# mLSTM head selectors made one head ahead, head 0's products of values spread over more steps, and a last norm in three vector steps with one product on GpSimd

## The chip, the cores and the metric

The kernel runs on one core of one Trainium2 chip. The time is device time of one execution in microseconds (us). The engines are TensorE (PE, matmuls), VectorE (DVE), ScalarE (ACT), GpSimd (POOL) and SyncE (SP, which issues DMAs here). In the code `T`, `V`, `S`, `G` and `nc.sync` stand for them in that order.

## The reference

A decoder block on 512 tokens of 1024 features with 16 learned tokens ahead, all in float32: a norm, one wide projection, an mLSTM mixer and a gated linear attention (GLA) mixer of 4 heads each beside each other, a gated merge, an output projection, a SwiGLU channel mixer, and a last norm. What the change touches is the mLSTM mixer and the last norm:

```python
dmat = jnp.where(causal, b[..., :, None] - b[..., None, :] + logi[..., None, :], -jnp.inf)
...
m_row = jnp.maximum(inter_log, jnp.max(dmat, axis=-1))
sim = jnp.einsum('bhcjd,bhcsd->bhcjs', q, k)
wts = jnp.exp(dmat - m_row[..., None]) * sim
...
den = a_inter * jnp.einsum('bhcd,bhcjd->bhcj', ns, q) + jnp.sum(wts, axis=-1)
return num / jnp.maximum(jnp.abs(den), jnp.exp(-m_row))[..., None]
...
out = rmsnorm(h, final_g)     # h * rsqrt(mean(h*h) + EPS) * final_g
```

## The kernel before, in words

Features lie on the 128 partitions and tokens along the free axis. A float32 product is made of three products of rounded halves: every weight is split into a high part (`whi`, a cast on ACT, L188) and a low part (`wlo`, a subtraction on DVE, L193), and so are the inputs. The projections of the mLSTM heads come first, one block of 128 columns after the other (`mm3`, L302 to L304). The later projections come in pairs by a scheme with seven products in place of eight (`seven` and `pair`, L344 to L346), in the order p7, q1, p3 of the pair before, q6, p4, p2, q5, of 12 matmuls each per half of the inner dimension. q1, q6 and q5 run in the same bank `bx`: between them ACT copies it out (`s1` L404 after q1, `s2` L405 after q6, `s5` L406 after q5), and the next of the three waits for its copy. `s7` (L407) and `c12` (L409) are two more such copies.

The order on every engine is the order in which the program is written; nothing reorders it. What lies beside the projections is written as generators: each `tick()`, called between the projections' matmuls (some 0.7 us of PE apart), moves every generator in `side` on by one step, and of the list `mixers` only the first, which holds the mLSTM heads 0 to 3 and then the GLA heads. `yield n` leaves n ticks before the next step. An earlier step of one head therefore brings forward all that follows in `mixers`, and its place among the projections with it.

All matmuls write into one pool of 8 banks of PSUM, taken by `bank()` in the program's order; a matmul into a bank waits until what the bank held before was read out. SBUF tiles of a tag wait in the same way.

A head (`mlstm`, L867) waits for its gates, queries and keys. It then makes a selector `sel` (L872), a matrix that picks this head's rows of the gate sums `gts.R`; two products with it (L875, L876) spread two gate rows over all partitions (`pb`, `pm`). ACT copies `pb` into `nml` (L879), DVE adds the causal mask (`dia`, L880), and for each of five chunks PE makes the scores (`sp`, L897 to L899), ACT the exponentials, DVE their product (L904), ACT and DVE its two halves `wh` and `wl` (L908, L917). When the values are there (transposed by PE, L748 and L766, read out by L752, L757, L769 and L774) follow the two halves of the product of values (`num`, L939 to L941), with the row sums (`den`, L944, L945) between, and the head's norm (`head_out`), which takes one more sum `ss` (L808, L809). `dh` and `dl` (L925, L930) are the halves of the row sums' input. The gates themselves come from `gate_rows`, which runs once, ahead of head 0; the convolution of queries and keys is L716.

`final(a, o)` is the last norm of column half a. `ones` times the squares gives their sum in a bank; ACT makes Ln and Exp (both L132, the line of the helper `act`) as a first guess of the inverse root, DVE improves it by a Newton step (L1488 to L1491), multiplies four blocks of two features each (L1495) and sends each off by a DMA (L1497). Half 0 runs while PE makes the last projection's second half; half 1 ends the program.

Of the kernel before, what the change touches and what calls it, by code (L numbers as in the profile page):

```python
# [9 lines left out]
F32R = mybir.dt.float32r  # L10
I32 = mybir.dt.int32
AF = mybir.ActivationFunctionType
ALU = mybir.AluOpType
PSUM = bass.MemoryType.PSUM

P = 128
D = 1024
KT = 8
NM = 16
NS = 512  # L20
NT = NM + NS
HALF = NT // 2
H = 4
DFF = 2816
FT = DFF // P
EPS = 1e-6
# [64 lines left out]
def jrange(c):  # L91
    return max(0, CH * c - NM), min(NS, CH * c + CH - NM)
# [8 lines left out]
def hybrid_block(ctx: ExitStack, tc: tile.TileContext, xT, wst, par, con, out):  # L101
    nc = tc.nc
    V, S, G, T = nc.vector, nc.scalar, nc.gpsimd, nc.tensor
# [3 lines left out]
    def nm(s):  # L107
        cnt[0] += 1
        return f"{s}_{cnt[0]}"
# [6 lines left out]
    def tt(dt=F32, n=NT, p=P):  # L116
        t = tpool.tile([P, TW], dt, tag="t", name=nm("t"))
        return t[:p, :n]

    def bank():  # L120
        return psum.tile([P, 512], F32, tag="b", name=nm("b"))
# [4 lines left out]
    def act(o, i, func, **kw):  # L126
        want = TABLE.get(func)
        if want is not None and want != table[0]:
            if want == LOGEXP:
                S.preload_act_table_set(want)  # L130
            table[0] = want
        S.activation(o, i, func, **kw)  # L132
# [288 lines left out]
    for k in range(KT):  # L421
        t = tt()
# [18 lines left out]
    cn = apool.tile([P, NS + 8], F32, name="cn")  # L441
# [3 lines left out]
    mpool = mpool_stack.enter_context(tc.tile_pool(name="mpool", bufs=1))  # L445
# [20 lines left out]
    for k in range(KT):  # L466
        g = pr[:, C_N1 + k:C_N1 + k + 1]
# [156 lines left out]
    gts = Box()  # L624
    gts.ready = False

    def gate_rows(ps):
        a2s = gts.a2s = apool.tile([P, 512], F32R, name="a2s")
        a2f = pr[:, C_A2:C_A2 + 512]
        gsb = tt()  # L630
        for a in range(2):
            c = slice(a * HALF, (a + 1) * HALF)
            V.tensor_tensor(gsb[:96, c], ps[0][a][:96], rstd[:96, c], ALU.mult)
        yield 16
        gam = gts.gam = tt(F32R)
        S.copy(gam[:96], gsb[:96])
        bi = pr[0:32, C_BG:C_BG + 1]
        bf = pr[32:64, C_BG:C_BG + 1]
        r1, r2, bl, a0 = tt(p=32), tt(p=32), tt(p=32), tt(p=32)
        act(r1, gsb[32:64], AF.Abs, bias=bf)  # L640
        yield 1
        act(r1, r1, AF.Exp, scale=-1.0)
        V.tensor_scalar(r2, gsb[32:64], bf, 0.0, op0=ALU.add, op1=ALU.min)
        yield 1
        act(r1, r1, AF.Ln, bias=b_one[:32])
        V.tensor_tensor(gam[64:96], gsb[64:96], gam[64:96].bitcast(F32), ALU.subtract)
        S.copy(a2s[:96], a2f[:96])
        yield 1
        V.tensor_tensor(r2, r2, r1, ALU.subtract)
        V.tensor_tensor_scan(bl, rmask[:32], r2, 0.0, ALU.mult, ALU.add)  # L650
        yield 1
        V.tensor_tensor(a2s[32:64], a2f[32:64], a2s[32:64].bitcast(F32), ALU.subtract)
        V.scalar_tensor_tensor(a0, gsb[0:32], bi, bl, ALU.add, ALU.subtract)
        yield 1
        d0, ml = r1, r2
        V.memset(d0, 0.0)
        V.tensor_copy(d0[:, CH::CH], bl[:, CH - 1:NT - 1:CH])
        V.tensor_tensor_scan(ml, d0, a0, 0.0, ALU.add, ALU.max)
        yield 1
        R = gts.R = tt(F32R, NS)  # L660
        mr = tt(p=32)
        rhi = d0
        act(R[0:32], ml[:, NM:], AF.Copy, scale=-1.0)
        V.tensor_tensor(mr, ml, bl, ALU.add)
        V.tensor_scalar(mr, mr, -1.0, 40.0, op0=ALU.mult, op1=ALU.min)
        yield 1
        V.scalar_tensor_tensor(R[32:64], ml[:, NM:], -1.0, R[0:32].bitcast(F32), ALU.mult, ALU.subtract)
        S.copy(R[64:96], mr[:, NM:])
        yield 1
        S.copy(rhi[:, NM:], R[64:96].bitcast(F32))  # L670
        yield 1
        V.tensor_tensor(R[96:128], mr[:, NM:], rhi[:, NM:], ALU.subtract)

        acol = gts.acol = apool.tile([P, 480], F32, name="acol")
        gts.idx = {}
        rows = [a0]
        n_ix = 0
        for d in range(NCK):
            if d > 0:
                nxt = tt(p=32)  # L680
                for i in range(NCK - d):
                    e = CH * (i + d) - 1
                    V.tensor_scalar(nxt[:, CH * i:CH * i + CH], rows[-1][:, CH * i:CH * i + CH], bl[:, e:e + 1],
                                    None, op0=ALU.add)
                rows.append(nxt)
            yield 2
        yield 8
        pst = bank()
        for d in range(NCK):
            n_ix = gate_cols(pst, rows, d, n_ix)  # L690
            yield 1
        yield 2
        V.tensor_copy(acol, pst[:, :480])
        gts.ready = True

    def gate_cols(pst, rows, d, n_ix):
        for i in range(NCK - d):
            w0, w1 = kwin(i)
            T.transpose(pst[:, n_ix * 32:n_ix * 32 + 32], rows[d][:, w0:w1], ident[:32, :32])
            gts.idx[(d, i)] = n_ix  # L700
            n_ix += 1
        return n_ix
# [161 lines left out]
    WTOT = off  # L864


    def mlstm(h, q, k, v, gates, dst):  # L867
        while not gts.ready or q.v is None or k.v is None:
            yield 1
        (qh, ql), (kh, kl) = q.v, k.v  # L870
        sel = mpool.tile([P, 2, P], F32R, tag="sel", name=nm("sel"))
        S.copy(sel, cn[:, NS + h:NS + 8:H].unsqueeze(2).to_broadcast([P, 2, P]))  # L872
        yield 6
        pb, pm = bank(), bank()
        T.matmul(pb, sel[:, 0], gts.R, start=True, stop=True)  # L875
        T.matmul(pm, sel[:, 1], gts.R, start=True, stop=True)  # L876
        yield 1
        nml, dia, em = tt(n=NS), tt(n=NS), tt(n=NS)
        S.copy(nml, pb)  # L879
        V.tensor_tensor(dia, pb, mask, ALU.add)  # L880
# [9 lines left out]
        for i in range(NCK + 1):  # L890
            cur = None
            if i < NCK:
                j0, j1 = jrange(i)
                w0, w1 = kwin(i)
                n = NS - j0
# [4 lines left out]
                e = tt(n=n)  # L900
# [27 lines left out]
        vh, vl = v.v  # L928
        yield 2
        V.tensor_tensor(dl, es, dh.bitcast(F32), ALU.subtract)  # L930
        yield 6
        den = bank()
        num = [bank(), bank()]
        for vt in range(2):
            for i in range(NCK):
                j0, o = jrange(i)[0], WOFF[i]
                n = NS - j0
                fi, la = i == 0, i == NCK - 1
                T.matmul(num[vt][:, j0:], vh(i, vt), wh[:, o:o + n], start=fi, stop=False)  # L939
                T.matmul(num[vt][:, j0:], vh(i, vt), wl[:, o:o + n], start=False, stop=False)  # L940
                T.matmul(num[vt][:, j0:], vl(i, vt), wh[:, o:o + n], start=False, stop=la)  # L941
            yield 1
            if vt == 0:
                T.matmul(den, onesr, dh, start=True, stop=False)  # L944
                T.matmul(den, onesr, dl, start=False, stop=True)  # L945
                act(nml, den, AF.Abs)
                yield 1
                V.tensor_tensor(em, nml, em, ALU.max)
                act(em, em, AF.Square)
# [156 lines left out]
    def head(kind, h):  # L1106
        if (kind, h) not in heads:
            b = heads[kind, h] = Box()
            b.q, b.k, b.v, b.vf, b.gates = box(), box(), box(), [box(), box()], [box(), box()]
            if kind == "m":  # L1110
                mix(mlstm(h, b.q, b.k, b.v, b.gates, ym))
                run(values(b.v, mtail, b.vf, h, True))
            else:
                dk = box()
                run(gla_decay(h, b.q, b.k, dk))
                mix(gla(h, dk, b.v, b.gates, yg))
                run(values(b.v, gtail, b.vf, h, False))
        return heads[kind, h]
# [178 lines left out]
    HS = NS // 2  # L1297
# [176 lines left out]
    def final(a, o):  # L1474
        yield 16
        ps = bank()[:, :HS]
        T.matmul(ps, ones, hsum[a].v, start=True, stop=False)
        while o.v is None:
            yield 1
        yield from out_res(7, o.v, a * HS, (a + 1) * HS)  # L1480
        yield 1
        T.matmul(ps, ones, hsum[a].w, start=False, stop=True)
        yield 1
        y, t = tt(n=HS), tt(n=HS)
        act(y, ps, AF.Ln, bias=b_eps, scale=1.0 / D)
        act(y, y, AF.Exp, scale=-0.5)
        yield 1
        V.tensor_tensor(t, y, y, ALU.mult)  # L1488
        V.scalar_tensor_tensor(t, ps, D * EPS, t, ALU.add, ALU.mult)
        V.tensor_scalar(t, t, -0.5 / D, 1.5, op0=ALU.mult, op1=ALU.add)  # L1490
        V.tensor_tensor(y, y, t, ALU.mult)  # L1491
        yield 1
        for j in range(4):
            g = hgain[j, a]
            V.tensor_tensor(g, g, y.unsqueeze(1).to_broadcast([P, 2, HS]), ALU.mult)  # L1495
            q = S if j % 2 else nc.sync
            q.dma_start(out[2 * j:2 * j + 2, :, a * HS:(a + 1) * HS].rearrange("m p n -> p m n"), g)  # L1497
            yield 1

# [109 lines left out]
```

## Time and profile before

| | |
|---|---|
| median of 3 runs | 948.26 us (947.28 to 948.26) |
| profiled execution | 948.52 us, span 946.7 us |
| granted clock of TensorE, mean | 0.992 |
| PE busy | 917.5 us, 97% of the span |
| DVE, ACT, POOL busy | 636.2, 546.2, 86.8 us |
| DMA moved | 124.45 MB, mean 131 GB/s |

In the rows below, a timeline row gives start, duration, engine, line, operation, names, tile shapes, count, and in brackets the idle time before it with what ended it. A row of waits gives the waiting line, what it waited for, total, count and longest. Times are us from the span's start.

### The profile page before, as it was taken

Reading aid. Unit: us, or ns where it says so; the run is one execution under the profiler, and the core shown is the slowest. Engines: PE = TensorE matmul, PEld = TensorE weight load, DVE = VectorE, ACT = ScalarE, POOL = GpSimd, SP = SyncE. Lnnn points to the kernel's source line nnn. Section 1 sums busy time; section 2 is a strip of 40 time slices with the busy share of each in tenths; the row PEclk is TensorE's granted clock in tenths of the full one; section 3 lists DMA queues with packets and bytes.
Section 4 is the critical chain, followed back from the end, with each engine's and each line's share of the span. In section 5 each row is a group of like instructions: output and inputs, shape, how many; then the busy total and the mean of one; then the engine's idle time right before and its main releaser. Section 6 shows DMA issues by size and latency. Waiting matters only on the chain.

```text
span 946.7 us, 15478 instructions
## 1 busy us (share of the span) xinstructions
PE 917.5 (97%) x6083; PEld 842.3 (89%) x6083; DVE 636.2 (67%) x940; ACT 546.2 (58%) x954; POOL 86.8 (9%) x102
## 2 busy tenths in 40 slices
PE   6999999989999999999999999999999999999995
PEld 6988899878998899999998888888999999888885
DVE  6797776767875577777777556785767767842323
ACT  7557788779684256766874334443555555732321
POOL 0000022001100011110100000212121110000000
PEclk9999999989999999999999999999999999999998
DMA  7245375345562466655643343335788885322302
GB/s 262 101 139 155 119 162 123 75 112 134 127 163 90 111 148 155 163 120 141 134 134 107 116 133 116 107 102 132 185 186 179 189 191 148 115 94 85 111 1 89
DMA packets 48712, 124.45 MB, mean 131 GB/s; under 512 B 5376, under 2 KB 11520, under 8 KB 48640
## 3 DMA queue, kind: packets, MB, share of 16 engines
q1 hardware_dynamic: 35008, 101.32, 34.5%
q0 software_dynamic: 12544, 21.11, 14.5%
q8 instruction: 47, 0.77, 0.3%
q10 hardware_dynamic: 1088, 1.05, 0.3%
q14 instruction: 25, 0.20, 0.1%
HBM read 118.08 MB, written 5.37 MB: 130 GB/s over the span
## 4 chain that ended last, share of the span: by engine, by line
PE 78%; ACT 9%; DVE 8%; issue 3%; DMA 1%; DVEq 0%; SPq 0%; ACTq 0%
PE b L303 13%; PE b L302 13%; PE b L304 13%; PE b L344 12%; PE b L345 11%; PE b L346 11%; ACT t L132 4%; ACT whi L188 2%; DVE wlo L193 1%; ACT L130 1%; PE b L1056 1%; DVE t L716 1%; PE b L1058 1%; PE b L1035 1%; ACT L132 1%
## 5 line engine op out<-in xcount | busy, mean ns | idle before, releaser
L303 PE MATMUL b<-t,whi 128*128 128x512 f32 (+2 forms) x822 | 289.9, 353 | 1.0 <-DVE t L471 0.7
L302 PE MATMUL b<-t,whi 128*128 128x512 f32 (+2 forms) x774 | 274.0, 354 | 6.7 <-ACT t L132 6.6
L304 PE MATMUL b<-t,wlo 128*128 128x512 f32 (+2 forms) x774 | 270.8, 350 | 0.0
L344 PE MATMUL b<-t,whi 128*128 128x256 f32 (+1 forms) x864 | 250.0, 289 | 7.7 <-ACT t L404 6.1
L346 PE MATMUL b<-t,wlo 128*128 128x256 f32 (+1 forms) x864 | 245.1, 284 | 0.0
L345 PE MATMUL b<-t,whi 128*128 128x256 f32 (+1 forms) x864 | 245.0, 284 | 0.0
L193 DVE TENSOR_TENSOR wlo<-raw,whi 128x1024 fp32r<-128x1024 f32 x155 | 193.1, 1249 | 50.8 <-ACT whi L188 50.5
L188 ACT CAST whi<-raw 128x1024 fp32r<-128x1024 f32 x155 | 161.7, 1047 | 64.5 <-PE b L345 27.4
L303 PEld LDWEIGHTS b<-t,whi 128*128 128x128 f32 x822 | 155.8, 190 | 23.3 <-DVE t L843 1.1
L344 PEld LDWEIGHTS b<-t,whi 128*128 128x128 f32 x864 | 164.3, 190 | 9.9 <-ACT t L404 7.2
L302 PEld LDWEIGHTS b<-t,whi 128*128 128x128 f32 x774 | 147.0, 190 | 26.5 <-ACT t L132 6.6
L345 PEld LDWEIGHTS b<-t,whi 128*128 128x128 f32 x864 | 164.3, 190 | 0.5
L304 PEld LDWEIGHTS b<-t,wlo 128*128 128x128 f32 x774 | 146.8, 190 | 19.9 <-DVE wlo L193 0.3
L346 PEld LDWEIGHTS b<-t,wlo 128*128 128x128 f32 x864 | 164.0, 190 | 0.0
L132 ACT ACTIVATE t<-t 128x512 f32<-128x512 f32 (+6 forms) x124 | 70.4, 588 | 29.8 <-DVE t L1289 9.3
L183 POOL DMA_DIRECT2D raw<-wst x36 | 31.2, 867 | 364.4 <-DMA wf<-wst 104.9
L188 ACT CAST whi<-wf 128x1024 fp32r<-128x1024 f32 x36 | 37.8, 1051 | 22.5 <-PE b L345 13.5
L132 ACT ACTIVATE t<-f 128x256 f32<-128x256 f32 (+1 forms) x24 | 11.6, 482 | 61.6 <-DVE f L1456 61.6
L212 POOL DMA_DIRECT2D wf<-wst x36 | 32.5, 912 | 155.3 <-DMA wf<-wst 85.7
L193 DVE TENSOR_TENSOR wlo<-wf,whi 128x1024 fp32r<-128x1024 f32 x36 | 43.9, 1218 | 0.0
L1456 DVE TENSOR_TENSOR f<-f,b 128x512 f32<-128x512 f32 (+1 forms) x9 | 5.7, 629 | 53.3 <-PE b L304 53.3
L344 PE MATMUL b<-t,wgh 128*128 128x256 f32 (+1 forms) x144 | 41.0, 285 | 0.0
(219 smaller groups left out, 1216.6 us busy)
## 6 DMA issues: line engine op xcount, KB each, us to landing
raw<-wst SPq DMA_DIRECT2D x155, 512.0 KB, 3.6
wf<-wst SPq DMA_DIRECT2D x36, 256.0 KB, 3.2
wf<-wst POOLq DMA_DIRECT2D x36, 256.0 KB, 5.4
raw<-wst POOLq DMA_DIRECT2D x36, 256.0 KB, 4.7
t<-xT SPq DMA_DIRECT2D x8, 264.0 KB, 5.6
pos<-t SPq DMA_DIRECT2D x8, 264.0 KB, 2.3
t<-xT SPq DMA_DIRECT2D x8, 256.0 KB, 3.8
t<-neg POOLq DMA_DIRECT2D x6, 272.0 KB, 6.3
```

The lines of the kernel that those rows point to most:

```text
L130: S.preload_act_table_set(want)
L132: S.activation(o, i, func, **kw)
L183: G.dma_start(lr(r, 0), lr(wst[v - 1], 0), accum_op=ALU.add)
L188: S.copy(t, src)
L193: V.tensor_tensor(t, src, hi.bitcast(F32), ALU.subtract)
L212: G.dma_start(lr(st.f, 1), lr(wst[u + 1], 1), accum_op=ALU.add)
L302: T.matmul(o, w_h, ah[:, c0:c1], start=first, stop=False)
L303: T.matmul(o, w_h, al[:, c0:c1], start=False, stop=False)
L304: T.matmul(o, w_l, ah[:, c0:c1], start=False, stop=last)
L344: T.matmul(o, h, xh_[k][:, c0:c1], start=start and k == 0, stop=False, skip_group_check=not start)
L345: T.matmul(o, h, xl_[k][:, c0:c1], start=False, stop=False, skip_group_check=not start)
L346: T.matmul(o, l, xh_[k][:, c0:c1], start=False, stop=k == 3, skip_group_check=not start)
```

## The change

`selector(h)` makes `gts.sel`, for head 0 in `gate_rows` behind `R`, for head h + 1 in head h behind its two products; the six ticks between selector and products are gone. In head 0 there are 8 ticks instead of 6 ahead of `den` and `num`, and 4 more between the halves of `num`. In `final`, the factor with the sum is made by one DVE operation beside ACT's Ln and Exp; the Newton step then takes three operations; the products are made in the order 2, 0, 1, 3, number 2 on GpSimd, and numbers 1 and 2 are sent from ACT's queue.

```diff
@@ gate_rows
         V.tensor_tensor(R[96:128], mr[:, NM:], rhi[:, NM:], ALU.subtract)
+        selector(0)
@@ mlstm
+    def selector(h):
+        gts.sel = mpool.tile([P, 2, P], F32R, tag="sel", name=nm("sel"), bufs=1)
+        S.copy(gts.sel, cn[:, NS + h:NS + 8:H].unsqueeze(2).to_broadcast([P, 2, P]))
+
...
-        sel = mpool.tile([P, 2, P], F32R, tag="sel", name=nm("sel"))
-        S.copy(sel, cn[:, NS + h:NS + 8:H].unsqueeze(2).to_broadcast([P, 2, P]))
-        yield 6
+        sel = gts.sel
         pb, pm = bank(), bank()
         T.matmul(pb, sel[:, 0], gts.R, start=True, stop=True)
         T.matmul(pm, sel[:, 1], gts.R, start=True, stop=True)
         yield 1
+        del sel
+        if h < H - 1:
+            selector(h + 1)
...
-        yield 6
+        yield 8 if h == 0 else 6
         den = bank()
         num = [bank(), bank()]
         for vt in range(2):
+            if h == 0 and vt:
+                yield 4
@@ final
+        y, t, x = tt(n=HS), tt(n=HS), tt(n=HS)
...
-        y, t = tt(n=HS), tt(n=HS)
+        V.tensor_scalar(x, ps, D * EPS, -0.5 / D, op0=ALU.add, op1=ALU.mult)
         act(y, ps, AF.Ln, bias=b_eps, scale=1.0 / D)
         act(y, y, AF.Exp, scale=-0.5)
         yield 1
         V.tensor_tensor(t, y, y, ALU.mult)
-        V.scalar_tensor_tensor(t, ps, D * EPS, t, ALU.add, ALU.mult)
-        V.tensor_scalar(t, t, -0.5 / D, 1.5, op0=ALU.mult, op1=ALU.add)
-        V.tensor_tensor(y, y, t, ALU.mult)
+        V.tensor_tensor(t, t, x, ALU.mult)
+        V.scalar_tensor_tensor(y, t, 1.5, y, ALU.add, ALU.mult)
         yield 1
-        for j in range(4):
+        for j in (2, 0, 1, 3):
             g = hgain[j, a]
-            V.tensor_tensor(g, g, y.unsqueeze(1).to_broadcast([P, 2, HS]), ALU.mult)
-            q = S if j % 2 else nc.sync
+            e = G if j == 2 else V
+            e.tensor_tensor(g, g, y.unsqueeze(1).to_broadcast([P, 2, HS]), ALU.mult)
+            q = S if j in (1, 2) else nc.sync
```

In the changed file the lines of `mlstm` stand 3 to 8 lower (pb L878, `nml` L885, `dia` L886, scores L903, casts L914, `num` L947, `den` L952), the convolution is L717, and the last products are L1504.

Three places show how the order moves. First ACT where head 0's selector was made in the kernel before; `cn` holds the constants, `b_866` is `pb`:

```order
L511 CAST t_791<-t_767 128x528
L132 ACTIVATE t_794<-t_767 128x272
L872 CAST sel_799<-cn 128x256
L752 CAST t_827<-b_816 128x512
L769 CAST t_844<-b_846 128x256
L132 ACTIVATE t_877<-t_862,pr 128x528
L879 COPY t_880<-b_866 128x512
```

and the same place in the changed kernel, where the selector is that of head 1 and `b_801` is `pb` of head 0:

```order
L511 CAST t_793<-t_769 128x528
L132 ACTIVATE t_796<-t_769 128x272
L870 CAST sel_812<-cn 128x256
L885 COPY t_814<-b_801 128x512
L130 ACT_TABLE_LOAD
L132 ACTIVATE t_816<-b_802,cb 128x512
L753 CAST t_840<-b_827 128x512
```

Head 0's own selector has gone 17 rows ahead, and the copy of `pb` stands ahead of the reading of head 1's transposed values (L753) instead of behind it.

Second ACT in the third pair, from its L404 to behind its L405. Before:

```order
L404 COPY t_2627<-b_2623 128x256
L407 COPY t_2628<-b_2622 128x256
L130 ACT_TABLE_LOAD
...
L132 ACT_TABLE_LOAD
L132 ACTIVATE t_2462<-t_2462 128x512
L132 ACTIVATE t_2463<-t_2463 128x512
L132 ACTIVATE t_2329<-b_2706 128x512
L405 COPY t_2628<-b_2623 128x272
L132 ACTIVATE t_2331<-t_2331 128x512
L130 ACT_TABLE_LOAD
```

and in the changed kernel, where `t_2758` is the norm's sum of head 3:

```order
L404 COPY t_2677<-b_2673 128x256
L407 COPY t_2678<-b_2672 128x256
L130 ACT_TABLE_LOAD
...
L132 ACT_TABLE_LOAD
L132 ACTIVATE t_2498<-t_2498 128x512
L132 ACTIVATE t_2499<-t_2499 128x512
L130 ACT_TABLE_LOAD
L132 ACTIVATE t_2599<-t_2758 128x512
L405 COPY t_2678<-b_2673 128x272
```

The reading of head 3's `den` (`b_2706`) is no longer there, and a table load and the norm's logarithm have come ahead of L405.

Third DVE in the last norm of half 1. Before:

```order
L1488 TENSOR_TENSOR t_9931<-t_9930 128x256
L1489 SCALAR_TENSOR_TENSOR t_9931<-b_9908,t_9931 128x256
L1490 TENSOR_SCALAR t_9931<-t_9931 128x256
L1491 TENSOR_TENSOR t_9930<-t_9930,t_9931 128x256
L1495 TENSOR_TENSOR t_9304<-t_9304,t_9930 128x512
L1495 TENSOR_TENSOR t_9404<-t_9404,t_9930 128x512
L1495 TENSOR_TENSOR t_9590<-t_9590,t_9930 128x512
L1495 TENSOR_TENSOR t_9772<-t_9772,t_9930 128x512
```

and in the changed kernel:

```order
L1493 TENSOR_SCALAR t_9912<-b_9909 128x256
L1497 TENSOR_TENSOR t_9911<-t_9910 128x256
L1498 TENSOR_TENSOR t_9911<-t_9911,t_9912 128x256
L1499 SCALAR_TENSOR_TENSOR t_9910<-t_9911,t_9910 128x256
L1504 TENSOR_TENSOR t_9304<-t_9304,t_9910 128x512
L1504 TENSOR_TENSOR t_9404<-t_9404,t_9910 128x512
L1504 TENSOR_TENSOR t_9772<-t_9772,t_9910 128x512
```

The third product (`t_9590`) is gone from DVE; it stands on GpSimd, behind nothing but the same product of half 0.

On PE, head 3's products with the selector and its scores stand ahead of the first pair instead of reaching into it, and its `num` and `den` in the second pair instead of the third.

## The prediction

> **What bounds the kernel now.** I read the page's busy line and chain first, then the list of what TensorE (PE) waits for, then the timeline around each of those waits.
>
> ```profile
> PE 917.5 (97%) x6083; PEld 842.3 (89%) x6083; DVE 636.2 (67%) x940; ACT 546.2 (58%) x954; POOL 86.8 (9%) x102
> PE 78%; ACT 9%; DVE 8%; issue 3%; DMA 1%; DVEq 0%; SPq 0%; ACTq 0%
> ...
> PE b L344 <- ACT t L404: 6.1, 4, 3.6
> PE b L875 <- ACT sel L872: 1.9, 1, 1.9
> PE b L939 <- DVE t L757: 1.6, 1, 1.6
> PE b L344 <- ACT t L405: 1.1, 1, 1.1
> PE b L748 <- ACT t L591: 0.5, 1, 0.5
> ```
>
> PE is busy for 917.5 of 946.7 us, so all idle time is 29.2 us, and the change can win only what PE waits for, or what lies behind PE's last product. The waits (total, count, longest) name its targets: the selector (L875), the second half of a product of values (L939), and the copies of the paired products (L404, L405), which come when head 3 ends. The profiled execution took 948.52 us (span 946.7 and 1.82 around it), 0.26 above the median of the runs, 948.26; the terms are differences against the profiled execution and are then taken from the median.
>
> **Head 0's selector.** These are rows of the timeline, of PE, DVE and ACT in turn.
>
> ```profile
> 67.20 0.28 PE L302 MATMUL b<-t,whi 128*128 128x264 f32 x1
> 69.60 0.50 PE L875 MATMUL b<-t,sel 128*128 128x512 f32 x1 [1.87 <-ACT sel L872]
> ...
> 68.72 1.53 DVE L716 SCALAR_TENSOR_TENSOR t<-t,pr,t 128x512 f32<-128x512 f32 x2
> ...
> 69.16 0.39 ACT L872 CAST sel<-cn 128x256 fp32r<-128x256 f32 x1
> ```
>
> The two products with the selector now come 12 triples of projection products earlier, near 62.4, and the wait of 1.87 is gone. But their banks must be emptied: the copy of the first (ACT, L885) stands behind the next selector's cast, which ends near 69.5, so it ends near 70.0; the masked sum (DVE, L886) stands behind L716, which ends at 70.25, so it ends near 70.9. The projection product that takes this bank ran at 67.20. With the two products with the selector (0.57) and three score products (0.69) ahead of it, and 0.7 of smaller waits for banks (pm's, and the scores' behind L593), PE reaches it near 69.15 and waits 1.75. New waits of 2.45 stand against the old 1.87 and 0.12 (at the first score product): +0.4, between −2.0 (no bank waits) and +0.9. The casts are the same four as before, at 0.39 each, in an ACT that idles there: 0.
>
> **Products of values and the transposes.** The wait at the second half of head 0's product of values:
>
> ```profile
> 104.09 0.47 PE L939 MATMUL b<-wh,t 128*128 128x512 f32 x1 [1.57 <-DVE t L757]
> ...
> 103.26 0.68 DVE L757 TENSOR_TENSOR t<-b,t 128x512 fp32r<-128x512 f32 x1
> ```
>
> Its bank is that of head 1's transposed values, read by DVE until 103.94. The longer steps (8 and 4) leave this half where it was among the projections, while the first half, den and its reading by ACT (Abs) are 3 to 5 us earlier; the bank it takes is now den's, free near 99.7. Gone: 1.57; one short wait near 97 of 0.18 goes too, and den's own second product may wait 0.2 for DVE: −1.55 (−1.75 to −0.6, the last if ACT reads den 1 us late). The wait of 0.45 at L748 goes, since its transposes now stand behind more PE work: −0.45 (0 at the other end). For heads 1 and 2 I find no wait at their places before and none after; 0, with 0.5 either way.
>
> **Head 3 and the four pairs.** Head 3's scores move from the first pairs to ahead of them, and its products of values from the third pair to the second.
>
> ```profile
> 179.90:199.30 19.40, 16.22 (x96) 14.03 (x94) 13.79 (x19) 16.52 (x31) 1.72 (x2) 0.97 0.35 86
> 199.30:214.70 15.40, 14.30 (x95) 13.91 (x95) 9.30 (x15) 10.77 (x27) 0.86 (x1) 0.81 0.34 98
> ...
> 199.71 0.58 PE L344 MATMUL b<-t,whi 128*128 128x256 f32 x1 [3.59 <-ACT t L404]
> 215.10 0.39 PE L344 MATMUL b<-t,whi 128*128 128x256 f32 x1 [1.09 <-ACT t L404]
> 221.07 0.38 PE L344 MATMUL b<-t,whi 128*128 128x256 f32 x1 [1.11 <-ACT t L405]
> 243.84 0.40 PE L344 MATMUL b<-t,whi 128*128 128x272 f32 x1 [0.88 <-ACT t L404]
> ```
>
> The columns of the windows are length, busy time (count) of PE, weight loads, DVE, ACT and GpSimd, granted clock, DMA share, GB/s. In the 19.4 us before the first copy L404 ACT works 16.5 and idles 2.9; the exponentials and casts of head 3 that move there from the next window, about 5.0 to 5.5 by their rows, fill this and 2.2 us more, so L404 comes at 201.5 instead of 199.29, and the product behind it 0.42 later, at 201.9. PE comes later too, since more of the score products (1.7) precede: at 197.8 instead of 196.1. The first wait is about 4.1 in place of 3.59, +0.5 (0 to +2, the latter if the casts wait for DVE as they do in the second window). In the second pair ACT then has 5.6 us between two L404 instead of the 10.65 it has in the second window, and PE has head 3's products between: both waits go, 1.09 + 1.11 = −2.2 (−1.1 at the worst). The fourth pair's 0.88 goes, some 0.4 of it back at a weight's low part: −0.5.
>
> The third pair had no wait, and gets one:
>
> ```profile
> 226.62 0.40 ACT L404 COPY t<-b 128x256 f32<-128x256 f32 x1
> 227.32 1.28 ACT L130 ACT_TABLE_LOAD   x1
> ...
> 230.82 1.28 ACT L132 ACT_TABLE_LOAD   x1
> ...
> 233.18 0.58 ACT L132 ACTIVATE t<-b 128x512 f32<-128x512 f32 x1
> 233.65 0.38 ACT L405 COPY t<-b 128x272 f32<-128x272 f32 x1
> ...
> 235.15 1.28 ACT L130 ACT_TABLE_LOAD   x1
> ...
> 227.99 0.39 PE L939 MATMUL b<-wh,t 128*128 128x512 f32 x1
> 232.27 0.40 PE L939 MATMUL b<-wh,t 128*128 128x512 f32 x1
> 236.81 0.29 PE L344 MATMUL b<-t,whi 128*128 128x272 f32 x1
> ```
>
> ACT is at L405 7.03 us after L404. In the changed order the activation at 233.18 is gone from between, and a table load (1.28) and a logarithm (0.53) stand there: 7.03 − 0.47 + 1.82 = 8.4, and 8.8 with L405 itself. PE needed it only at 236.81, because 4.9 us of head 3's products stood between (two halves from 227.99 and 232.27, of 15 matmuls and 2.2 us each, and den's two of 0.5). In the changed order PE has from the end of the product that L404 copies only four groups of 12 matmuls at 0.118 (24 in 2.80 us, in the row at 205.20 below) and two for a norm: 48 × 0.118 + 0.45 = 6.1. So PE waits 8.8 − 6.1 = +2.7 (0 if the copies and loads slip ahead of it, +3.5 at most, if L404 itself is late).
>
> The clock adds a risk:
>
> ```profile
> 199.50:202.00 2.50, 2.29 (x10) 2.29 (x11) 0.67 (x1) 2.29 (x8) 0.00 (x0) 0.50 1.05 235
> 202.00:205.20 3.20, 3.20 (x15) 3.01 (x15) 1.31 (x3) 0.67 (x2) 0.00 (x0) 0.51 0.29 113
> 205.20:208.00 2.80, 2.80 (x24) 2.80 (x24) 1.72 (x3) 2.38 (x5) 0.00 (x0) 1.00 0.00 0
> 70.00:74.00 4.00, 3.88 (x28) 3.49 (x27) 4.00 (x9) 0.29 (x2) 0.00 (x0) 1.00 0.58 166
> ```
>
> Behind the wait of 3.59 the clock was half for 5.5 us, a loss of 2.7; behind that of 1.87 (last row) it was full. The first wait stays long, so its loss stays; a third-pair wait of 2.7 lies between the two lengths, and I leave it at full clock. The Trainium skill ("TensorE: Matmul & The Clock Gate", What's actually happening) has the clock halved by an idle window of about 3.4 us, free-running; by that page 2.7 us would not fill one, so the sum would stand and the slower rival below would fall away, and the wait of 3.59 would fill one only where its phase is right. The row at 70 agrees for 1.87; no run here shows 2.7.
>
> **The last norm.** Only the second column half ends the program.
>
> ```profile
> 939.84 0.29 DVE L1490 TENSOR_SCALAR t<-t 128x256 f32<-128x256 f32 x1
> 940.16 0.43 DVE L1491 TENSOR_TENSOR t<-t,t 128x256 f32<-128x256 f32 x1
> 940.62 2.50 DVE L1495 TENSOR_TENSOR t<-t,t 128x512 f32<-128x512 f32 x4
> ...
> 610.38 4.55 POOL L1294 TENSOR_TENSOR t<-t,t 128x512 f32<-128x512 f32 x1 [6.64 <-ACT t L132]
> 631.56 1.59 POOL L1294 TENSOR_TENSOR t<-t,t 128x512 f32<-128x512 f32 x1 [0.71 <-DVE t L1290]
> ...
> 631.92 2.32 DVE L193 TENSOR_TENSOR wlo<-raw,whi 128x1024 fp32r<-128x1024 f32 x1
> 606.62 1.21 DVE L193 TENSOR_TENSOR wlo<-raw,whi 128x1024 fp32r<-128x1024 f32 x1
> ```
>
> L1490's place leaves the path (−0.32); its successor, read from the bank, lies beside ACT's Ln and Exp. DVE's four products of 0.62 become three, so alone they would end at 942.2 instead of 943.1. But beside a GpSimd product of 1.59 the same DVE subtraction took 2.32 instead of 1.21: it stood still until GpSimd was done. So in the tail the second DVE product waits: GpSimd 940.45 to 942.05, the second product to 942.65, the third to 943.2, as before. The tail is then +0.1; −0.7 if the two run side by side (GpSimd's transfer, then j=1's behind it on ACT's queue, set the end). In the row at 610.38 it is GpSimd that stood still, 4.55 us behind five back-to-back DVE operations; then its transfer and j=1's behind it come last: +0.6 to +1.0. The first half's tail lies beside PE's last products; 0. The Trainium skill ("GPSIMD Engine Reference", Engine selection and Key points) advises VectorE for two-input elementwise work, GpSimd being about half as fast and sharing its interfaces with DVE instructions of two inputs; the rows at 631 agree. By that page the tail gains nothing and the sum is −1.0; without contention it would be −1.8.
>
> **Sum.** +0.4 − 1.55 − 0.45 + 0.5 − 2.2 − 0.5 + 2.7 + 0.1 = −1.0. From 948.26: 947.3.
>
> **Rivals.**
> - The pairs gain freely: the third pair's wait doesn't come, because ACT is ahead there, or the first wait breaks into shorter ones ahead of the pairs and the clock stays full (2.7 either way). For: ACT has 5 us less to do behind L404. Against: three table loads lie between L404 and L405. 948.26 − 1.0 − 2.7 = 944.6. Chance 0.25.
> - The selector's wait goes without bank waits in its place. For: PE's early products meet an idle DVE at 66.6 to 67.5. Against: the copy and the sum stand behind work that ends at 70. 947.3 − 2.4 = 944.9. Chance 0.12.
> - Slower: the third pair's wait of 2.7 halves the clock as the wait of 3.59 did. It decides from the idle length at which the clock falls, between 1.87 and 3.59. 947.3 + 2.7 = 950.0; with a first wait of 5.5, 951.4. Chance 0.15.
> - The gains are given back at once (the selector at +0.9, den read late, tail locked out): 948.3, no change; it counts to my own case's spread.
>
> **Numbers.** My sum has 0.48, with a range of its own from 946.0 to 948.9. A change of under 0.2% (1.9 us) is about what measurement can't tell from none: faster is below 946.4, slower above 950.2. The first two rivals hold 0.37, and the sum's lower edge 0.05: faster 0.42. The slower rival lies on the bound; half of it and the sum's upper edge give 0.13; same 0.45. The range from 943.8 to 950.2 takes in each rival by itself, and leaves out the first two together and the slower one with a long first wait.
>
> **What would show it.** No wait at L878 and one of 1 to 2 us at a projection product near 70, released by DVE L886; none at L947 in head 0; a first wait at L344 of about 4 with half clock behind it; none in the second pair; one of 2 to 3 us behind L405 in the third; a DVE product L1504 of about 1.7 us beside GpSimd's. It is wrong if L405's wait is absent, if the clock stays full near 200, or halves a second time.

## The result, and the profile after

The changed kernel is slower: 949.61 us (median of 20 runs, 948.85 to 951.04) against 947.25 us for the kernel before (20 runs, 945.64 to 948.51). The ratio is 1.0026, with a 95% interval of 1.002 to 1.0032. The forecast was 947.3 from a median of 948.26 over 3 runs, a gain of 1.0; measured is a loss of 2.4. The profiled execution of the changed kernel has a span of 947.6 us, that of before 946.7; its 948.52 us lie just above the highest of before's 20 runs, so two single executions show less of the loss than the medians.

The page's busy line and PE's waits of the changed kernel (total, count, longest):

```profile
PE 916.8 (97%) x6083; PEld 841.6 (89%) x6083; DVE 637.7 (67%) x938; ACT 546.5 (58%) x954; POOL 90.2 (10%) x104
```

```profile
PE b L344 <- ACT t L404: 6.5, 2, 6.0
PE b L344 <- ACT t L405: 3.0, 2, 2.6
PE b L302 <- DVE t L886: 1.3, 1, 1.3
PE b L953 <- DVE t L936: 0.9, 1, 0.9
PE b L303 <- DVE t L844: 0.3, 1, 0.3
PE b L903 <- DVE t L593: 0.2, 1, 0.2
```

The wait at the selector (1.87), at head 0's second half (1.57) and at L748 (0.45) are gone. A bank wait behind L886 (1.3) and one of head 2's `den` (0.9) are new, the longest wait at L404 has grown from 3.6 to 6.0, and L405 has a wait of 2.6. The timeline shows where, PE first, then ACT:

```profile
70.50 0.39 PE L302 MATMUL b<-t,whi 128*128 128x264 f32 x1 [1.35 <-DVE t L886]
201.76 0.58 PE L344 MATMUL b<-t,whi 128*128 128x256 f32 x1 [6.00 <-ACT t L404]
223.69 0.39 PE L344 MATMUL b<-t,whi 128*128 128x256 f32 x1 [0.45 <-ACT t L405]
237.60 0.59 PE L344 MATMUL b<-t,whi 128*128 128x272 f32 x1 [2.58 <-ACT t L405]
...
201.34 0.36 ACT L404 COPY t<-b 128x256 f32<-128x256 f32 x1
228.69 0.40 ACT L404 COPY t<-b 128x256 f32<-128x256 f32 x1
235.35 1.28 ACT L130 ACT_TABLE_LOAD   x1
236.64 0.63 ACT L132 ACTIVATE t<-t 128x512 f32<-128x512 f32 x1
237.18 0.37 ACT L405 COPY t<-b 128x272 f32<-128x272 f32 x1
```

The first copy L404 starts at 201.34 instead of 199.29, and between the third pair's L404 and L405 lie 8.49 us, the table load at 235.35 and the logarithm at 236.64 among them. The clock behind both waits, in windows (length, busy time and count of PE, weight loads, DVE, ACT, GpSimd, granted clock, DMA share, GB/s):

```profile
201.00:208.00 7.00, 6.24 (x35) 6.24 (x36) 4.14 (x12) 3.64 (x9) 0.00 (x0) 0.62 0.47 112
...
235.00:237.60 2.60, 0.02 (x2) 0.01 (x1) 0.48 (x3) 2.57 (x5) 0.00 (x0) 0.89 0.90 148
237.60:241.00 3.40, 3.40 (x17) 3.40 (x18) 2.62 (x4) 3.37 (x8) 0.00 (x0) 0.58 0.00 1
241.00:245.00 4.00, 4.00 (x34) 4.00 (x33) 4.00 (x8) 2.94 (x7) 0.00 (x0) 1.00 0.12 16
```

In 237.60 to 241.00 PE made 17 products where the same length at full clock holds some 29 (34 in 4.00): the clock was halved a second time in this execution, a loss of some 1.4 us. The end of the program:

```profile
937.57 0.70 PE L1491 MATMUL b<-t,ones 128*128 128x256 f32 x2 [0.96 <-ACT t L132]
...
938.31 0.42 DVE L1493 TENSOR_SCALAR t<-b 128x256 f32<-128x256 f32 x1 [1.24 <-PE b L1491]
938.77 0.47 ACT L132 ACTIVATE t<-b,cb 128x256 f32<-128x256 f32 x1 [0.85 <-DVE t L1493]
...
941.10 2.96 DVE L1504 TENSOR_TENSOR t<-t,t 128x512 f32<-128x512 f32 x3
941.21 1.70 POOL L1504 TENSOR_TENSOR t<-t,t 128x512 f32<-128x512 f32 x1 [6.49 <-DVE t L1499]
```

ACT's Ln waits 0.85 for DVE's reading of the same bank, and three DVE products beside GpSimd's take 2.96 where four took 2.50. From the end of PE's last product (938.27 here, 937.92 before) to the end of DVE's last one it is 5.79 us instead of 5.20; to the end of the span it is 9.3 instead of 8.8.

### The profile page after: what moved, and what is told of

Its sections match the earlier page's. It is cut to its first block, busy times and chain, and to the rows that moved or that the text cites. A ratio compares the mean times of both kernels' runs of the same rounds, so it can differ in the third digit from the quotient of the medians.

```text
span 947.6 us, 15476 instructions
## 1 busy us (share of the span) xinstructions
PE 916.8 (97%) x6083; PEld 841.6 (89%) x6083; DVE 637.7 (67%) x938; ACT 546.5 (58%) x954; POOL 90.2 (10%) x104
## 4 chain that ended last, share of the span: by engine, by line
PE 82%; ACT 8%; DVE 6%; issue 2%; DMA 1%; SPq 0%; DVEq 0%; ACTq 0%
PE b L303 13%; PE b L302 13%; PE b L304 13%; PE b L344 12%; PE b L345 12%; PE b L346 12%; ACT t L132 3%; DVE wlo L193 1%; ACT whi L188 1%; PE b L1064 1%; ACT L130 1%; DVE t L717 1%; PE b L1066 1%; PE b L1043 1%; ACT L132 1%
## 5 line engine op out<-in xcount | busy, mean ns | idle before, releaser
L344 PE MATMUL b<-t,whi 128*128 128x256 f32 (+1 forms) x864 | 249.8, 289 | 10.1 <-ACT t L404 6.5
```

Of the source, the lines that this page charges most:

```text
L344: T.matmul(o, h, xh_[k][:, c0:c1], start=start and k == 0, stop=False, skip_group_check=not start)
```

## The experiments

Times are medians, each against the runs of the kernel before on the same chip (947.2 to 947.5 in the four sets); ratios are to these, with their 95% intervals.

### The tail alone, and the change without it

`tail_only` is the kernel before with the changed `final`, `old_tail` the changed kernel with the old one.

> The kernel before with the new last norm alone. In the changed kernel's trace the end of the program, from PE's last product on, takes 9.33 us instead of 8.77: Ln waits for DVE's reading of the same bank, and three DVE products take 2.96 beside GpSimd's 1.70 where four took 2.50. Theory 'stage' (the tail's own loss, the rest of the slowdown from the pairs): +0.6 us against the kernel before. Rival 'tail is harmless' (0.56 is an accident of one execution): 0 or -0.3, the removed step.

> The changed kernel with the last norm of before. Theory 'stage': 0.6 us faster than the changed kernel, so still some +1.8 against the kernel before, with the first wait near 6.0 and the third pair's near 2.6 unchanged. Rival 'the tail is the cause': within 0.5 us of the kernel before.

`tail_only` took 947.65 us, ratio 1.0003 (0.9994 to 1.0012): timing can't tell it from no change. Its trace shows the 5.79 us again, so the 0.59 is no accident of one execution. `old_tail` took 949.89 us, 1.0021 (1.0012 to 1.003), with waits of 6.00 and 2.58; the 0.6 us that it should have gained on the changed kernel don't show in its time. The slowdown doesn't come from the tail.

### Head 3 put back to its old place

```diff
         sel = gts.sel
+        if h == H - 1:
+            yield 18
         pb, pm = bank(), bank()
```

> The changed kernel with 18 more steps ahead of head 3's products with the selector, so that head 3 stands among the projections where it stood in the kernel before; heads 0 to 2 and the tail stay changed. Theory 'stage' (head 3's earlier place loads ACT ahead of the first pair, and takes the cover from the third pair): the first wait falls from 6.0 to 4 to 5 with PE's earlier gains still paid back in it, no wait at the third pair's L405 and no half clock there, the second pair's two waits of 1.1 come back; 2 to 3 us faster than the changed kernel, -0.5 to +0.5 against the kernel before. Rival 'head 3's place costs nothing by itself': as the changed kernel, +2.4 against before. If the earlier gains of heads 0 to 2 are not paid back but stay: -1.5 to -2 against before.

943.57 us, ratio 0.9958 (0.9946 to 0.9971): 6.0 us faster than the changed kernel and 3.6 faster than the kernel before. The step that costs is head 3's earlier place. More came than either theory gave: the gains of heads 0 to 2 stay, and the second pair's waits don't come back. PE's waits in the pairs are now two:

```profile
198.56 0.44 PE L344 MATMUL b<-t,whi 128*128 128x256 f32 x1 [3.92 <-ACT t L404]
238.41 0.40 PE L344 MATMUL b<-t,whi 128*128 128x272 f32 x1 [0.70 <-ACT t L404]
```

The windows over the whole stage, of the kernel before, the changed one, and this one:

```profile
176.00:260.00 84.00, 77.32 (x545) 73.18 (x546) 62.90 (x103) 65.73 (x131) 10.45 (x13) 0.96 0.48 114
```
```profile
176.00:260.00 84.00, 74.97 (x526) 71.32 (x526) 59.06 (x93) 64.30 (x124) 10.50 (x13) 0.94 0.46 116
```
```profile
176.00:260.00 84.00, 79.38 (x582) 75.85 (x582) 64.12 (x100) 68.03 (x129) 10.47 (x13) 0.98 0.53 129
```

PE is busy for 77.32, 74.97 and 79.38 of the 84 us, at a clock of 0.96, 0.94 and 0.98. Head 3 stands among the projections exactly where it stood in the kernel before. Head 2 stands earlier, so its norm (`ss`, 48 matmuls of projections earlier) no longer falls into the pairs; that this is why the second pair's waits stay away is likely, but no run changed it alone.

### PE kept busy in the two waits

```diff
+        if n_pair[0] == 1:
+            warm(by, w, x, *cols, 40)      # 40 products of 128x256 into by, which p2 overwrites
         seven(bx, w, x, "q6", False, hook, *cols)
...
+        if n_pair[0] == 3:
+            warm(by, w, x, *cols, 18)
         seven(by, w, x, "p2", True, hook, *cols)
```

> The changed kernel with products that nobody reads put into the two waits (40 of 128x256 before q6 of the first pair, 18 before p2 of the third, into a bank that the next product overwrites), so that PE isn't idle there. Theory 'clock' (the half clock behind the two waits, 0.62 over 7 us and 0.58 over 3.4 us, costs some 2.7 and 1.4): the clock stays at 1.00 through 200 to 245 and the kernel is 2.5 to 4 us faster than the changed one, so 0 to -1.5 against before. Rival 'the slow clock lies under ACT's work and costs nothing': as the changed kernel within 0.5, or slower by what the added products take (up to 0.5).

947.54 us, ratio 1.0003 (0.9994 to 1.0012), 2.1 us less than the changed kernel, for 58 products more. The clock stayed at 1.00 through 200 to 245 in its profile, and waits of 1.35 and 0.32 are left at the two places. The half clock does cost, though less than the 2.5 to 4 expected. The waits' own length stays, since the added products only fill it.

### Head 3's norm behind the third pair's copy

```diff
+        if hd == H - 1 and gcol == C_MG:
+            yield 8
         act(y0, x, AF.Ln, scale=1.0 / 256.0)
```

> The changed kernel with 8 more steps between head 3's sum ss and its logarithm, so that the logarithm and the table load ahead of it stand behind the third pair's L405 on ACT again; nothing else moves. Theory 'third pair' (this table load and the backlog behind it cost the 2.58 wait and the half clock after it): L405 comes some 1.8 us sooner, its wait falls to 0.5 to 1.0, the clock stays full there, the first wait stays at 6.0; 2 to 3.3 us faster than the changed kernel, so -1 to +0.4 against the kernel before. Rival 'only the first wait matters': 0 to -0.8 against the changed kernel.

948.97 us, ratio 1.0013 (1.0004 to 1.0022), only 0.6 us less than the changed kernel. The third pair's wait fell from 2.58 to 0.63 as foreseen, with full clock, but the fourth pair got one:

```profile
201.78 0.58 PE L344 MATMUL b<-t,whi 128*128 128x256 f32 x1 [6.00 <-ACT t L404]
236.00 0.39 PE L344 MATMUL b<-t,whi 128*128 128x272 f32 x1 [0.63 <-ACT t L405]
239.91 0.40 PE L346 MATMUL b<-t,wlo 128*128 128x272 f32 x1 [0.39 <-DVE wlo L193]
243.94 0.39 PE L344 MATMUL b<-t,whi 128*128 128x272 f32 x1 [0.99 <-ACT t L404]
```
```profile
230.00:245.00 15.00, 12.99 (x99) 12.33 (x98) 10.91 (x17) 14.83 (x27) 2.68 (x4) 1.00 0.60 157
```

ACT is busy for 14.83 of 15 us there. A table load taken from ahead of one copy stands ahead of the next.

### The added steps at head 0 alone

```diff
-        yield 6
+        yield 8 if h == 0 else 6
...
+            if h == 0 and vt:
+                yield 4
```

> The kernel before with the 8 and the 4 steps at head 0's products of values alone; since the selectors keep their 6 steps, heads 1 to 3 now come later among the projections than before (head 3's selector products 24 matmuls later). Theory 'place' (what an mLSTM head's place among the pairs does to ACT decides; the wait at head 0's second half is real): the wait of 1.57 near 104 goes, and head 3's later place takes some of the load off ACT ahead of the first pair: -1.5 to -3 against before. Rival 'paid back' (whatever PE gains ahead of 176 us goes into the first wait): -0.5 to +0.5, with the first wait longer by as much.

949.71 us, ratio 1.0023 (1.0014 to 1.0031): slower by 2.5, against both theories. The wait of 1.57 is gone, but with the selectors' six steps still there heads 1 to 3 come later, and the pairs get five waits: 2.55, 1.13, 1.72, 0.35 and 1.75. Later isn't better either: the place decides, with a price on both sides.

### The selectors ahead, at the old places

This is the kernel before with `selector(0)` in `gate_rows`, `selector(h + 1)` in `mlstm`, and `yield 6` kept ahead of the two products.

> The kernel before with the selectors made one head ahead, but the 6 steps ahead of the products kept, so that every product stands where it stood; old tail. Theory 'the selector's wait is real and its cover is place': PE's wait of 1.87 at the selector falls to 0 to 1, since ACT's cast is done long before but the banks and DVE stay as they are; -0.9 to -1.9 at 70 us, of which the first wait takes a part: -0.3 to -1.9 in all. Rival 'paid back whole': -0.3 to +0.3.

948.58 us, ratio 1.0011 (1.0001 to 1.0021), in runs from 946.94 to 951.55. In the trace the wait at the selector's product has fallen from 1.87 to 0.82, now ended by DVE (`acol`), and a wait of 1.10 stands at the head's first score product, behind the reading of head 1's transposed values (DVE L758):

```profile
68.99 0.50 PE L880 MATMUL b<-t,sel 128*128 128x512 f32 x1 [0.82 <-DVE acol L694]
72.79 0.50 PE L904 MATMUL b<-t,t 128*128 128x512 f32 x1 [1.10 <-DVE t L758]
```

At the 480th projection product (counted from the 40th) nothing is left of the gain. The early selector by itself brings nothing.

### Selectors ahead and head 3 back, without the added steps

```diff
+        if h == H - 1:
+            yield 22
...
-        yield 8 if h == 0 else 6
+        yield 6
```

(and the four steps between the halves taken out)

> The changed kernel without the added steps at head 0's products of values, and with head 3 held back to its place in the kernel before (22 steps): selectors ahead, heads 1 and 2 still earlier. Theory 'places': the wait of some 1.5 at head 0's second half may come back, heads 1 and 2 gain as with the steps; -1.5 to -3.5 against before. Rival 'the added steps carry the gain of the version held back': -0.5 to -1.5 only.

940.65 us, ratio 0.9933 (0.992 to 0.9947), in five runs from 940.22 to 942.30. The added steps cost some 3 us where head 3 stands back: without them head 1 and head 2 come earlier still, PE's wait at the first pair is 2.57, and the clock in the profiled execution, the fastest of the five, was full through the whole stage:

```profile
196.70 0.39 PE L344 MATMUL b<-t,whi 128*128 128x256 f32 x1 [2.57 <-ACT t L404]
234.98 0.39 PE L344 MATMUL b<-t,whi 128*128 128x272 f32 x1 [0.65 <-ACT t L404]
```
```profile
176.00:260.00 84.00, 80.79 (x608) 77.25 (x607) 65.54 (x101) 69.64 (x133) 11.27 (x14) 1.00 0.54 132
```

### Half the way back

`h3_mid` is `h3_back` with 9 steps in place of 18.

> The changed kernel with head 3 held back by 9 steps, half of the 18 that brought it to its old place. Theory 'load ahead of the first pair': the first wait lies between 6.0 and 3.92, head 3's products of values in the second or third pair decide the rest; 944 to 948 in all. Rival 'a threshold' (either the head's work fits ahead of the first copy or not): near 943.6 or near 949.6.

948.89 us, ratio 1.0013 (1.0004 to 1.0022), neither near 944 nor in the middle. The first wait is 3.85, as with 18 steps, and waits of 1.64 (third pair, L405) and 2.69 (fourth pair, L404) follow, with a clock of 0.67 in 200 to 208. Half the steps bring nearly the whole gain at the first pair and lose it at the next ones.

### Work taken off ACT ahead of the first copy

`act_relief` makes the eight copies L580 on DVE, `act_pool` on GpSimd, both in the changed kernel.

> The changed kernel with the eight copies L580 (2.9 us of ACT between 184 and 188) on DVE, which idles some 6 us there; no order among the products changes. Theory 'ACT bounds the stage from 176 to 202': L404 comes 1.5 to 2.9 us sooner, the first wait falls from 6.0 to 3.1 to 4.5, and the kernel is 1.5 to 2.9 us faster than the changed one (0 to +1 against before). Rival 'L404 waits for something else, DVE or head 3's scores': first wait 5.5 to 6.5, same time as the changed kernel or slower.

> The changed kernel with the eight copies L580 on GpSimd, which does nothing then, in place of ACT; DVE gets no added work (on DVE the copies made ACT wait 1.80 and 1.43 for it, more than the 2.9 they took off). Theory 'ACT's work ahead of L404 sets the first wait': L404 1.5 to 2.9 us sooner, first wait 3.1 to 4.5, 1.5 to 2.9 us faster than the changed kernel. Theory 'head 3's chain of exponential, product and cast between ACT and DVE sets it': first wait 5.5 to 6.3, no faster.

950.73 us (1.0032, 1.002 to 1.0043) and 950.27 us (1.0029, 1.0018 to 1.0041): not faster than the changed kernel, first waits of 6.19 and 6.11. What was taken off ACT came back as waits of ACT. The first three rows are of `act_pool`, where ACT waits 2.10 for GpSimd's copies and 0.74 for DVE; the other three are the same instructions in the changed kernel:

```profile
187.99 0.41 ACT L132 ACTIVATE t<-t,acol 128x128 f32<-128x128 f32 x1 [2.10 <-POOL t L580]
189.13 0.62 ACT L914 CAST wh<-t 128x512 fp32r<-128x512 f32 x1 [0.74 <-DVE t L910]
202.41 0.36 ACT L404 COPY t<-b 128x256 f32<-128x256 f32 x1
```
```profile
187.78 0.40 ACT L132 ACTIVATE t<-t,acol 128x128 f32<-128x128 f32 x1
188.09 0.60 ACT L914 CAST wh<-t 128x512 fp32r<-128x512 f32 x1
201.34 0.36 ACT L404 COPY t<-b 128x256 f32<-128x256 f32 x1
```

From head 3's first cast L914 to L404 it is 13.28 us in both (13.25 in the changed kernel), with ACT idle for at most 0.34 at a time. L404 follows the cast by 13.3 us of ACT's own work in all three, and in `h3_back`, where head 3's exponentials and casts are not in that stretch, it comes 3.2 us sooner. What less work ahead of that cast would bring, these two runs don't show, since their ACT waited about as long as it had been relieved. In the changed kernel itself the stretch from 176.00 to L404 leaves ACT almost no idle time:

```profile
176.00:201.34 25.34, 19.76 (x113) 16.96 (x112) 18.56 (x31) 24.70 (x52) 2.60 (x3) 0.96 0.34 84
```

It is busy for 24.70 of the 25.34 us, so there the sum of its work sets L404. No run took work out of this stretch and left head 3's place alone.

### The last norm taken apart

`h3_tail_order` is `h3_back` with DVE's reading written behind ACT's Ln; GpSimd keeps its product.

> The changed kernel with head 3 held back, and in the last norm DVE's reading of the sum's bank written behind ACT's Ln instead of ahead of it; GpSimd's product stays. One look at the end of the program. Theory 'two causes': from PE's last product to DVE's last one takes 5.3 us instead of 5.79 (Ln no longer waits 0.85 for DVE), and 4.87 is left to the version without GpSimd, so GpSimd's product costs 0.45 and the order of the readers 0.45. Rival 'GpSimd alone': 5.7 to 5.8. Rival 'order alone': 4.9.

In its one execution (942.57 us) it is 5.33 us from PE's last product to DVE's last, against 5.79 with the changed tail and 4.87 with all four products on DVE (below). The order of the two readers costs 0.46, GpSimd's product another 0.46, and the removed step is worth 0.33 against the 5.20 of before.

### The fastest form

`h3_warm` is `h3_back` with 28 unread products in its first wait, `best` adds the last norm on DVE alone with the readers' order turned, `best2` is `h3_sel` with 16 such products and that last norm.

> The changed kernel with head 3 held back by 18 steps, and 28 products that nobody reads (3.3 us) in the remaining first wait of 3.92. Theory 'clock': full clock behind it (0.86 over 200 to 208 becomes 1.00), 1 to 2.5 us faster than without them, 941 to 942.5 in all. Rival: the slow stretch is covered by ACT's work, and waits at the second pair come in its place: 0 to -0.5.

> As the one before (head 3 held back, 28 products in the first wait), with a last norm in which DVE reads the bank behind ACT's Ln instead of ahead of it, and makes all four last products, sent as in the kernel before; the three Newton operations stay. Theory 'order of two readers' (Ln waited 0.85 for DVE's reading, and three products beside GpSimd's took as long as four and more): the end of the program from PE's last product on takes 8.4 to 8.5 us instead of 9.33 with the changed tail and 8.77 with the old one; 0.8 us faster than without, within what timing can show. Rival 'the readers don't hinder each other': 9.0 to 9.3.

> The version with head 3 held back and the old steps at head 0's products of values (940.65), with 16 products that nobody reads (1.9 us) in its first wait of 2.57 and the last norm of DVE alone with the readers' order turned. Theory: the two slow runs of five there (942.1, 942.3) were half clock behind the first wait and go; the tail gives 0.9: 939.2 to 940.0 with less spread.

`h3_warm` took 942.04 us (0.9938, 0.9924 to 0.9951), 1.5 less than without the products. `best` took 940.86 (0.9926, 0.9914 to 0.9939), with 4.87 us from PE's last product to DVE's last. `best2` took 939.48 us, ratio 0.9914 (0.9899 to 0.9929), in runs from 939.01 to 939.73: 10.1 us faster than the changed kernel and 8.0 faster than the kernel before. In its rows L413 is the copy `s1`, which is L404 in the changed kernel:

```profile
197.11 0.38 PE L344 MATMUL b<-t,whi 128*128 128x256 f32 x1 [0.73 <-ACT t L413]
235.41 0.39 PE L344 MATMUL b<-t,whi 128*128 128x272 f32 x1 [0.65 <-ACT t L413]
...
931.86 2.50 DVE L1512 TENSOR_TENSOR t<-t,t 128x512 f32<-128x512 f32 x4
```

## Why the prediction was wrong

| step | predicted | measured in the changed kernel's trace |
|---|---|---|
| selector of head 0 | 1.99 goes, 2.45 comes | 1.99 goes, 1.60 comes (1.35 behind L886, 0.25 behind L593) |
| products of values of head 0, L748 | −1.55, −0.45 | 1.57, 0.18 and 0.45 gone |
| heads 1 and 2 | 0 | 0.91 at head 2's `den` |
| first copy L404 | at 201.5 | at 201.34 |
| PE arrives at the first pair | at 197.8 | at 195.76 |
| first wait | 4.1 | 6.00 |
| second pair | both waits go | 0.45 left of 2.20 |
| third pair, L404 to L405 | 8.4 | 8.49 |
| third pair's wait | 2.7 | 2.58 |
| clock behind it | full | half for 3.4 us in this execution |
| fourth pair | 0.4 left | none |
| last norm | +0.1 | +0.59 |

The measured terms are of one execution each and needn't add up to the difference of the medians; the executions are also shifted a little from the start (the 300th projection product runs at 53.52 us in the kernel before, at 53.13 in the changed one, at 53.64 in `h3_back`).

**The failed step is the first wait.** That head 3's work fills ACT's idle time and pushes L404 back was right. This is the changed kernel's stretch up to its L404:

```profile
179.90:201.34 21.44, 15.86 (x89) 13.52 (x87) 16.62 (x28) 20.98 (x45) 1.72 (x2) 0.96 0.34 91
```

ACT works 20.98 of 21.44 us there, where it worked 16.52 of 19.40 before: 4.46 more work (5.0 to 5.5 forecast) and 2.42 less idle time (2.9 forecast), so L404 is 2.05 later (2.2 forecast). It is placed within 0.2 us partly by luck, since the two errors, each of half a microsecond or more, cancel. But PE's arrival was put 1.7 us later than before for the score products moved ahead of it, and the sum then counted the gains ahead of it, 1.55 and 0.45, as gains of the whole. They bring PE to the same place that much earlier, and L404 didn't come earlier with it. So the wait took them back: it is 6.00, or 1.9 more than the 4.1 of the sum, about the 2.0 that were counted as kept. `h3_back` shows the other side: with the same gains at heads 0 to 2, head 3 where it was before and L404 at 198.15 instead of 199.29, PE arrives at 194.64 instead of 196.12 and waits only 0.33 longer than before. There the gains stay.

**The third pair's wait came as worked out, and with it the slower rival,** which had 0.15: the clock was half behind a wait of 2.58, which the sum left at full clock. It doesn't come every time: in `old_tail`, the same program up to the last norm, the same 2.58 left the clock at 1.00 from 237.16 to 245. The prediction looked for an idle length between 1.87 and 3.59 at which the clock falls; the runs show none, for in `tail_only` the selector's wait of 1.87 itself was followed by half the clock (last section). That it was full behind the same wait in the kernel before, on which the sum built, was chance. A second halving was one of the prediction's own signs of being wrong, and it came. The gain from holding the clock in both waits is 2.1 us (`warm`).

**The second pair:** ACT's work between the two copies L404 was put at 5.6 us against 10.65 before; the prediction's own row has 10.77, and the changed kernel's trace 6.17. The wait behind L404 went, as foreseen, and of that behind L405 (1.11) 0.45 was left.

**The last norm:** that DVE's reading of the bank would lie beside Ln and Exp was wrong. Ln waited for it, a price of 0.46. The products beside GpSimd went as foreseen (DVE's second stood still, three took 2.96). That rule of the Trainium skill was borne out: "GPSIMD Engine Reference", Engine selection, advises VectorE for such work, and the product on GpSimd cost 0.46.

**The base:** the terms were differences to one execution whose first wait was followed by 5.5 us of half clock. Over 20 runs the kernel before has a median 1.3 us under that execution, while the changed kernel's profiled execution (949.47) lies at its own median. How often the kernel before escapes the full loss was not in the page, and the sum took none of it.

The rivals that ended faster failed: the third pair's wait came, and the selector's bank wait too.

## What to carry to other kernels

Waits removed ahead of a point that another engine sets are not added to the sum: first ask when that engine releases the point, then subtract. Work moved ahead in one chain moves everything behind it in the chain, so a change of place should be undone for the last link alone before it is judged: here a delay of 18 steps turned a loss of 2.4 us into a gain of 3.6, and 9 steps left a loss. A second reader of a bank goes behind the one on the critical path.

## What the runs showed of the hardware

How long PE waits doesn't tell whether its clock drops. A wait of 3.41 us left it at 1.00, and behind one of 1.75 it fell to 0.76 over 7 us. First `ahead_only`, then `num_only`, a row of PE and one of the windows each:

```profile
200.30 0.38 PE L344 MATMUL b<-t,whi 128*128 128x256 f32 x1 [3.41 <-ACT t L404]
```
```profile
200.30:208.00 7.70, 7.70 (x61) 7.62 (x62) 5.08 (x8) 6.90 (x17) 0.00 (x0) 1.00 0.48 128
```
```profile
227.91 0.39 PE L344 MATMUL b<-t,whi 128*128 128x272 f32 x1 [1.75 <-ACT t L404]
```
```profile
227.90:235.00 7.10, 7.08 (x43) 7.09 (x44) 5.80 (x9) 7.04 (x15) 2.67 (x4) 0.76 0.75 175
```

What does tell is how the wait lies in time. In the 17 traces every stretch at half clock inside the program (from 20 to 930 us) is 3.41, 6.83 or 10.24 us long, so one, two or three times 3.41. Call this length a window, and lay windows end to end from a step of the clock. The kernel before and `tail_only` are one program up to the last norm, with the same wait of 1.87 at the selector. The first two rows are of `tail_only`, the last two of the kernel before, cut into such windows:

```profile
66.93:70.34 3.41, 1.54 (x11) 1.37 (x11) 3.38 (x5) 2.65 (x6) 0.00 (x0) 1.00 0.28 57
70.34:73.75 3.41, 3.41 (x15) 3.22 (x15) 3.25 (x8) 0.45 (x1) 0.00 (x0) 0.50 0.46 175
...
65.20:68.62 3.42, 2.52 (x21) 2.31 (x20) 2.53 (x7) 2.53 (x5) 0.00 (x0) 1.00 0.55 214
68.62:72.03 3.41, 2.43 (x18) 2.34 (x19) 3.37 (x6) 1.67 (x5) 0.00 (x0) 1.00 0.46 109
```

In `tail_only` the whole wait fell into one window, PE was busy for only 1.54 of its 3.41 us, and the next window ran at half clock. In the kernel before the edge of a window cut the wait in two, and the clock stayed full. Cut in this way, all 17 traces have 15 windows at full clock that a halved one follows, and in each PE was idle for 51% or more; of the windows followed by full clock only one (`ahead_only`, 53%) had as much. So in this kernel it takes about half of one window idle, and where the windows lie differs from one execution to the next: the wait of 2.58 left PE 1.39 busy in one window of the changed kernel's trace (halved), and 1.92 and 2.34 in two windows of `old_tail` (full).

The same stage differs between executions, too: behind its wait of 3.58 the kernel with the changed tail alone had 0.81 over the 9.03 us from 198.97, where the kernel before had 0.70 over 9.03 us from 199.71, a difference of 1.0 us in two programs that are equal up to there. "TensorE: Matmul & The Clock Gate" (What's actually happening) of the Trainium skill has a free-running window of some 3.4 us, which fits that the length alone doesn't decide, and the steps of 3.41 us; that it takes an idle window of that length is not what these rows show, since 1.75 and 2.58 were followed by a halved clock.
